# Twelve taps of a depthwise convolution as diagonal matrix products, and a chunk state whose decay is scaled ahead

## The chip, the cores and the metric

The kernel runs on one core of one Trainium2 chip. The metric is the device time of one execution in microseconds (us), taken as the median over several runs. Five engines work from queues of their own, each strictly in the order in which the program was written out: TensorE (PE in the profile, its weight loads PEld), VectorE (DVE), ScalarE (ACT), GpSimd (POOL) and SyncE (SP, which only issues transfers).

## The reference, cut to what matters

Two transformer blocks are computed for 512 tokens of width 1024. The change touches the first half of the first block: a causal depthwise convolution of 31 taps, and a linear recurrence over 16 heads of width 64.

```python
def conformer_conv(val, glu, conv_w, conv_vec):
    u = val * jax.nn.sigmoid(glu)
    y = lax.conv_general_dilated(u, conv_w, window_strides=(1,), padding=[(30, 0)],
                                 dimension_numbers=('NWC', 'WIO', 'NWC'), feature_group_count=1024)
    y = y + conv_vec[0]
    y = layer_norm(y, conv_vec[1], conv_vec[2], LN_EPS)
    return jax.nn.silu(y)

def rwkv7_step(state, inp):
    r_t, w_t, k_t, v_t, kk_t, a_t = inp
    sa = jnp.einsum('bhvk,bhk->bhv', state, -kk_t)
    state = (state * w_t[:, :, None, :] + sa[..., None] * (kk_t * a_t)[:, :, None, :]
             + v_t[..., None] * k_t[:, :, None, :])
    return state, jnp.einsum('bhvk,bhk->bhv', state, r_t)
```

Each channel of the convolution has its own 31 weights; nothing is summed over channels. The rest (attention with an index of selected keys, a short convolution, a large table of experts, a gate) is not touched.

## The kernel before

Channels lie on the 128 partitions and the 512 tokens along the free dimension, so 1024 channels are eight tiles of 128 x 512. The stage in question (function `even`) walks through a list of steps, `ORDER`:

- `A0` to `A7` (`rwkv_a`): the projections r, k, v of one pair of heads, the decays, and the matrices that each chunk of 64 tokens needs.
- `B0` to `B7` (`rwkv_b`): for each pair, a triangular inverse by 31 short steps of a product (line 660) and a reduction (line 662). For pairs 0 and 3 the product is on GpSimd, else on VectorE.
- `C0` to `C7` (`rwkv_c`): the recurrence, eight chunks one after the other. In each chunk PE makes X from the state S of the chunk before (line 705), VectorE copies X (708), PE makes U (712), ScalarE copies U (715), PE makes the new contributions `sy` (718 to 724), and VectorE updates the state: line 730 adds `sy` to S, line 731 multiplies the sum by the chunk's decay `PC`, one scalar per partition. ScalarE then copies the output chunk to `Y` (734).
- `c0` to `c7` (`conv_tile`): one tile of the convolution. Two projections (value and gate) go through PE into banks of PSUM named `mm`, and VectorE makes `u` from them (765), 30 zeros ahead of it. Taps 0 to 10 are multiplied on ScalarE (768 and 771, each 128 x 512 with one scale per partition) and summed on GpSimd into `p2` (772, ten additions). Tap 11 starts `y` on VectorE (778), taps 12 to 30 are added there one by one (780, 19 instructions), and line 783 adds `p2`. The tile goes out to DRAM, and GpSimd keeps a running sum `cs` (787, 789).
- afterwards `n` (normalisation), `g` (gates), `s` and `o` (the first half of the output projection).

All large products split each operand into a high and a low part of a faster 32-bit format, and make three products of them (`product`, lines 216 to 218). Matrices in plain float32 are multiplied without a split; the trace shows such a product of 128 x 512 as two records.

The order of the instructions on each engine is not the written one. A planner in the kernel file (`Order`) builds the program once, estimates each instruction, makes several list schedules of the whole program from priorities of the longest remaining way, and imposes the one with the shortest estimate (`impose`). Any change in one place can thereby move instructions everywhere.

Of the kernel before, what the change touches and what calls it, by code (L numbers as in the profile page):

```python
# [10 lines left out]
F32 = mybir.dt.float32  # L11
# [4 lines left out]
AF = mybir.ActivationFunctionType  # L16
OP = mybir.AluOpType
AX = mybir.AxisListType

T = 512  # L20
# [113 lines left out]
class Net:  # L134
# [253 lines left out]

    NP = 11
    HP = 0  # L390
# [301 lines left out]
    def rwkv_c(self, j):  # L692

        nc, I, wk = self.nc, self.I, self.wk
# [3 lines left out]
        for c in range(8):  # L698
# [27 lines left out]
            if c < 7:  # L726
                S2 = S
                S = wk.tile([128, 64], F32, name="S", bufs=2)
                if c:
                    nc.vector.tensor_tensor(S2, sy[:, 0], S2, OP.add)  # L730
                    nc.vector.tensor_scalar(S, S2, PC[:, c:c + 1], None, op0=OP.mult)
                else:
                    nc.vector.tensor_scalar(S, sy[:, 0], PC[:, c:c + 1], None, op0=OP.mult)
# [24 lines left out]
    def conv_tile(self, j):  # L758
# [6 lines left out]
        nc.vector.scalar_tensor_tensor(u[:, 30:], sg, 1.0, pv, op0=OP.add, op1=OP.mult)  # L765
        NP = self.NP
        p2 = wk.tile([128, T], F32, name="p2")
        nc.scalar.activation(p2, u[:, 0:T], AF.Identity, scale=self.hw[:, 31 * j:31 * j + 1], bias=self.V("conv_b", j))
        for k in range(1, NP):
            pr = wk.tile([128, T], F32, name="pr", bufs=2)  # L770
            nc.scalar.activation(pr, u[:, k:k + T], AF.Copy, scale=self.hw[:, 31 * j + k:31 * j + k + 1])
            nc.gpsimd.tensor_tensor(p2, p2, pr, OP.add)
        y = self.act.tile([128, T], F32, name=f"x{j % 2}")
        if self.CF:
            nc.vector.scalar_tensor_tensor(y, u[:, NP:NP + T], self.hw[:, 31 * j + NP:31 * j + NP + 1], p2,
                                           op0=OP.mult, op1=OP.add)
        else:
            nc.vector.tensor_scalar(y, u[:, NP:NP + T], self.hw[:, 31 * j + NP:31 * j + NP + 1], None, op0=OP.mult)
        for k in range(NP + 1, 31):
            nc.vector.scalar_tensor_tensor(y, u[:, k:k + T], self.hw[:, 31 * j + k:31 * j + k + 1], y,  # L780
                                           op0=OP.mult, op1=OP.add)
        if not self.CF:
            self.eng(5).tensor_tensor(y, y, p2, OP.add)
        nc.sync.dma_start(self.yad[j], y)
# [1120 lines left out]
```

## Time and profile before

| | us |
|---|---|
| median of 3 runs | 2883.79 (2883.66 to 2886.31) |
| the profiled execution | 2893.17 |
| its span, first to last instruction | 2891.4 |
| the stage of the change, 70 to 790 us | 720 |
| PE / DVE / ACT / POOL busy in it | 629 / 537 / 409 / 335 |
| PE clock granted in it, mean | 0.83 of full |

The stage of the change is read here as 70 to 790 us of the span: from the end of the first norm to the end of the eighth recurrence (`C7`). Convolution and recurrences run side by side in it until about 650 us; from 690 us on, gates, output projections and `C7` are left. What follows is the rest of the output projection (to 885), attention (to about 1450), the choice of experts (to 1900) and the experts themselves. The chain of waits that the page shows reaches back over the last 53% of the span only and says nothing of this stage, so the stage has to be read from busy times by stretch, from instruction groups and from waits. PE counts as busy until the modelled end of each product, about 0.2 us longer than the next product has to wait.

### The profile page before, as it was taken

Reading aid. Unit: us, or ns where it says so; the run is one execution under the profiler, and the core shown is the slowest. Engines: PE = TensorE matmul, PEld = TensorE weight load, DVE = VectorE, ACT = ScalarE, POOL = GpSimd, SP = SyncE. Lnnn points to the kernel's source line nnn. Section 1 sums busy time; section 2 is a strip of 40 time slices with the busy share of each in tenths; the row PEclk is TensorE's granted clock in tenths of the full one; section 3 lists DMA queues with packets and bytes.
Section 4 is the critical chain, followed back from the end, with each engine's and each line's share of the span. In section 5 each row is a group of like instructions: output and inputs, shape, how many; then the busy total and the mean of one; then the engine's idle time right before and its main releaser. Section 6 shows DMA issues by size and latency. Waiting matters only on the chain.

```text
span 2891.4 us, 45285 instructions
## 1 busy us (share of the span) xinstructions
PE 2621.8 (91%) x14523; PEld 2231.9 (77%) x14523; DVE 2247.7 (78%) x4338; ACT 1474.0 (51%) x3068; POOL 1852.7 (64%) x1942
## 2 busy tenths in 40 slices
PE   5788998879979999999999988769999999999996
PEld 3656655656757787877878787669999999999995
DVE  6688679896367999973669969978877778788865
ACT  6536546556635538975454347723333444433435
POOL 4535646452245553346657788869988899998963
PEclk9759888888989999999999999979999999999988
DMA  8635444445694231123334366699999999999971
GB/s 264 161 66 118 98 95 107 93 99 126 145 289 143 76 96 44 46 93 105 96 102 148 101 201 245 254 316 337 321 329 314 300 340 339 334 345 320 325 245 64
DMA packets 353440, 552.23 MB, mean 191 GB/s; under 512 B 60081, under 2 KB 239153, under 8 KB 351538
## 3 DMA queue, kind: packets, MB, share of 16 engines
q1 hardware_dynamic: 224690, 295.22, 32.1%
q0 software_dynamic: 64800, 201.88, 23.5%
q10 hardware_dynamic: 63712, 52.24, 5.7%
q8 instruction: 114, 1.87, 0.3%
q14 instruction: 124, 1.02, 0.1%
HBM read 507.76 MB, written 41.42 MB: 190 GB/s over the span
## 4 chain that ended last, share of the span: by engine, by line
PE 31%; DVE 11%; issue 4%; POOL 4%; DMA 2%; ACT 1%; DVEq 0%; POOLq 0%; ACTq 0%; SPq 0%
PE mm L216 5%; PE mm L218 5%; PE mm L217 5%; PE xu L1258 2%; PE xu L1256 2%; PE xu L1257 2%; PE tp L1256 1%; PE tp L1258 1%; POOL wl L209 1%; PE tp L1257 1%; PE nb L1258 1%; PE nb L1256 1%; POOL grow L1330 1%; PE nb L1257 1%; DVE o L1511 1%
## 5 line engine op out<-in xcount | busy, mean ns | idle before, releaser
L209 POOL TENSOR_TENSOR wl<-wraw,wh 128x256 fp32r<-128x256 f32 x937 | 776.7, 846 | 349.3 <-ACT wh L207 290.4
L207 ACT ACTIVATE wh<-wraw 128x256 fp32r<-128x256 f32 x937 | 367.5, 413 | 466.2 <-PE mm L217 235.1
L216 PE MATMUL mm<-xh,wh 128*128 128x352 f32 (+1 forms) x1464 | 512.1, 350 | 11.2 <-DVE wwl L242 3.5
L218 PE MATMUL mm<-xh,wl 128*128 128x352 f32 (+1 forms) x1464 | 506.1, 349 | 6.7 <-POOL wl L209 6.7
L217 PE MATMUL mm<-xl,wh 128*128 128x352 f32 (+1 forms) x1464 | 507.9, 348 | 2.7 <-DVE xl L287 1.8
L216 PEld LDWEIGHTS mm<-xh,wh 128*128 128x128 f32 x1464 | 278.7, 190 | 33.8 <-DVE gate L1544 4.3
L218 PEld LDWEIGHTS mm<-xh,wl 128*128 128x128 f32 x1464 | 277.4, 190 | 26.5 <-POOL wl L209 8.6
L217 PEld LDWEIGHTS mm<-xl,wh 128*128 128x128 f32 x1464 | 278.5, 190 | 24.2 <-DVE xl L287 3.8
L1240 POOL TENSOR_TENSOR vl<-vraw,vh 128x1024 fp32r<-128x1024 f32 x96 | 231.2, 2416 | 6.0 <-ACT vh L1236 4.4
L192 POOL DMA_DIRECT2D dl<-in_wev x114 | 102.4, 917 | 201.7 <-ACT dl L191 180.5
L1345 DVE SCALAR_TENSOR_TENSOR gscr<-grow,wide 128x1024 bf16<-128x1024 f32 x160 | 194.1, 1213 | 38.3 <-DMA grow<-in_ue,gidx 34.8
L216 PE MATMUL mm<-xh,dh 128*128 128x512 f32 x456 | 205.5, 453 | 14.9 <-ACT xh L355 9.6
L1361 DVE SCALAR_TENSOR_TENSOR wide<-grow,gdot,wide 128x1024 f32<-128x1024 f32 x158 | 202.3, 1280 | 12.3 <-DMA grow<-in_ev,gidx 11.2
L217 PE MATMUL mm<-xl,dh 128*128 128x512 f32 x456 | 202.7, 446 | 9.2 <-DVE xl L356 9.2
L218 PE MATMUL mm<-xh,dl 128*128 128x512 f32 x456 | 202.0, 446 | 9.1 <-DMA dl<-in_wev 9.1
L1330 POOL DMA_INDIRECT grow<-in_ue,gidx x160 | 161.1, 1007 | 64.7 <-DVE gscr L1345 31.1
L1256 PE MATMUL xu<-wwh,vh 128*128 128x352 f32 x512 | 167.4, 328 | 32.2 <-ACT wwh L241 28.0
L1330 POOL DMA_INDIRECT grow<-in_ev,gidx x160 | 157.4, 984 | 36.1 <-issue 23.5
L1258 PE MATMUL xu<-wwh,vl 128*128 128x352 f32 x512 | 167.4, 328 | 9.7 <-POOL vl L1240 7.7
L1191 ACT ACTIVATE mm<-mm 128x352 f32<-128x352 f32 x96 | 43.0, 448 | 253.0 <-PE mm L218 211.4
L1257 PE MATMUL xu<-wwl,vh 128*128 128x352 f32 x512 | 167.2, 327 | 0.4 <-DVE wwl L242 0.4
L780 DVE SCALAR_TENSOR_TENSOR x<-u,vec,x 128x512 f32<-128x512 f32 x152 | 165.6, 1089 | 2.4
(575 smaller groups left out, 6961.2 us busy)
## 6 DMA issues: line engine op xcount, KB each, us to landing
vraw<-in_ev SPq DMA_DIRECT2D x128, 512.0 KB
wraw<-in_uT SPq DMA_DIRECT2D x494, 128.0 KB
draw<-in_wev SPq DMA_DIRECT2D x114, 256.0 KB
dl<-in_wev POOLq DMA_DIRECT2D x114, 256.0 KB
gs<-st SPq DMA_DIRECT2D x11, 2048.0 KB
g<-gs ACTq DMA_DIRECT2D x32, 704.0 KB
wraw<-in_wod SPq DMA_DIRECT2D x156, 128.0 KB
adaw<-in_adaT SPq DMA_DIRECT2D x32, 512.0 KB
```

The costliest lines, as they stand in the source:

```text
L207: nc.scalar.activation(wh, raw[:, s], AF.Copy)
L209: nc.gpsimd.tensor_tensor(wl, raw[:, s], wh.bitcast(F32), OP.subtract)
L216: nc.tensor.matmul(ps, wh, xh, start=start, stop=False)
L217: nc.tensor.matmul(ps, wh, xl, start=False, stop=False)
L218: nc.tensor.matmul(ps, wl, xh, start=False, stop=stop)
L1240: nc.gpsimd.tensor_tensor(l, raw, h.bitcast(F32), OP.subtract)
L1256: nc.tensor.matmul(po, vh[i][:, s], wh[i], start=(i == 0), stop=False)
L1257: nc.tensor.matmul(po, vh[i][:, s], wl[i], start=False, stop=False)
L1258: nc.tensor.matmul(po, vl[i][:, s], wh[i], start=False, stop=(i == len(wh) - 1))
L1330: self.nc.gpsimd.indirect_dma_start(out=t, out_offset=None, in_=src, in_offset=bass.IndirectOffsetOnAxis(ap=self.gidx[i][:, k:k + 1], axis=0))
L1345: nc.vector.scalar_tensor_tensor(scr, u, 1.0, x, op0=OP.mult, op1=OP.mult, accum_out=self.gdot[i][:, k:k + 1])
L1361: nc.vector.scalar_tensor_tensor(acc, r, w, acc, op0=OP.mult, op1=OP.add)
```

## The change

`NP` goes from 11 to 12, and the first twelve taps move to PE. ScalarE makes for each tap a diagonal matrix (128 x 128) by scaling the identity with the tap's weight, one scale per partition; four matrices share one buffer, and there are two buffers. PE multiplies each matrix, as plain float32, with the shifted window of `u` and accumulates the twelve products in one bank of `mm`. ScalarE brings the sum out of PSUM with the bias added, as the start of `y`. VectorE then adds taps 12 to 30 as before. The additions on GpSimd, the first tap on VectorE and the final addition of `p2` are gone.

In the recurrence, ScalarE computes `S2`, the old state times the decay, ahead of time; VectorE then makes the new state in one instruction, `sy` times the decay plus `S2`.

```diff
             if c < 7:
-                S2 = S
+                if c:
+                    S2 = wk.tile([128, 64], F32, name="S2", bufs=2)
+                    nc.scalar.activation(S2, S, AF.Copy, scale=PC[:, c:c + 1])
                 S = wk.tile([128, 64], F32, name="S", bufs=2)
                 if c:
-                    nc.vector.tensor_tensor(S2, sy[:, 0], S2, OP.add)
-                    nc.vector.tensor_scalar(S, S2, PC[:, c:c + 1], None, op0=OP.mult)
+                    nc.vector.scalar_tensor_tensor(S, sy[:, 0], PC[:, c:c + 1], S2, op0=OP.mult, op1=OP.add)
...
-        p2 = wk.tile([128, T], F32, name="p2")
-        nc.scalar.activation(p2, u[:, 0:T], AF.Identity, scale=self.hw[:, 31 * j:31 * j + 1], bias=self.V("conv_b", j))
-        for k in range(1, NP):
-            pr = wk.tile([128, T], F32, name="pr", bufs=2)
-            nc.scalar.activation(pr, u[:, k:k + T], AF.Copy, scale=self.hw[:, 31 * j + k:31 * j + k + 1])
-            nc.gpsimd.tensor_tensor(p2, p2, pr, OP.add)
+        NP, ps = self.NP, self.bank("mm")
+        for k0 in range(0, NP, 4):
+            dg = wk.tile([128, T], F32, name="pr", bufs=2).rearrange("p (k c) -> p k c", c=128)
+            for k in range(k0, k0 + 4):
+                nc.scalar.activation(dg[:, k - k0], self.C("ident"), AF.Copy, scale=self.hw[:, 31 * j + k:31 * j + k + 1])
+            for k in range(k0, k0 + 4):
+                nc.tensor.matmul(ps, dg[:, k - k0], u[:, k:k + T], start=(k == 0), stop=(k == NP - 1))
         y = self.act.tile([128, T], F32, name=f"x{j % 2}")
...
-            nc.vector.tensor_scalar(y, u[:, NP:NP + T], self.hw[:, 31 * j + NP:31 * j + NP + 1], None, op0=OP.mult)
-        for k in range(NP + 1, 31):
+        nc.scalar.activation(y, ps, AF.Identity, bias=self.V("conv_b", j))
+        for k in range(NP, 31):
...
-        if not self.CF:
-            self.eng(5).tensor_tensor(y, y, p2, OP.add)
```

In the changed file the new instructions stand on lines 772 (diagonals), 774 (products), 776 (the sum out of PSUM), 729 (`S2`) and 732 (the state); the taps on VectorE are line 778 there and line 780 before, `u` is 766 and 765.

The planner's order changes with it, in three places that matter below. On VectorE, around the making of `u` for convolution tile 3 (`x_3766` and `x_3771` are its `y`). Before:

```order
L675 STREAM_TRANSPOSE T_4047<-Tt 32x256
L765 SCALAR_TENSOR_TENSOR u<-sg,mm 128x512
L778 TENSOR_SCALAR x_3766<-u,vec 128x512
L780 SCALAR_TENSOR_TENSOR x_3766<-u,vec,x_3766 128x512
L730 TENSOR_TENSOR S<-xu,S 128x64
L780 SCALAR_TENSOR_TENSOR x_3766<-u,vec,x_3766 128x512
L731 TENSOR_SCALAR S<-S,PC 128x64
L780 SCALAR_TENSOR_TENSOR x_3766<-u,vec,x_3766 128x512 x2
L708 COPY Xs<-xu 128x64
```

With the change:

```order
L766 SCALAR_TENSOR_TENSOR u<-sg,mm 128x512
L708 COPY Xs<-xu 128x64
L662 TENSOR_REDUCE Tp<-Ltmp 128x8
L660 TENSOR_TENSOR Ltmp<-Tp,Lp 128x8x31
L662 TENSOR_REDUCE Tp<-Ltmp 128x8
L660 TENSOR_TENSOR Ltmp<-Tp,Lp 128x256
L662 TENSOR_REDUCE Tp<-Ltmp 128x8
L732 SCALAR_TENSOR_TENSOR S<-xu,PC,S_3504 128x64
L708 COPY Xs<-xu 128x64
L675 STREAM_TRANSPOSE T_4046<-Tt 32x256 x2
L778 SCALAR_TENSOR_TENSOR x_3771<-u,vec,x_3771 128x512
L732 SCALAR_TENSOR_TENSOR S<-xu,PC,S_3528 128x64
```

Before, the first tap on VectorE stands right behind `u`; with the change nine rows of other work stand between them, and the two state instructions have become one.

On VectorE, at tile 4 (`x_3905` is its `y` in both). Before:

```order
L765 SCALAR_TENSOR_TENSOR u<-sg,mm 128x512
L780 SCALAR_TENSOR_TENSOR x_3766<-u,vec,x_3766 128x512
L778 TENSOR_SCALAR x_3905<-u,vec 128x512
L780 SCALAR_TENSOR_TENSOR x_3905<-u,vec,x_3905 128x512 x2
L730 TENSOR_TENSOR S<-xu,S 128x64
```

With the change:

```order
L778 SCALAR_TENSOR_TENSOR x_3771<-u,vec,x_3771 128x512 x3
L766 SCALAR_TENSOR_TENSOR u<-sg,mm 128x512
L745 SCALAR_TENSOR_TENSOR x_3648<-xu,Y 128x512
L778 SCALAR_TENSOR_TENSOR x_3905<-u,vec,x_3905 128x512 x16
L546 SCALAR_TENSOR_TENSOR k<-mm,om,tm 128x512
```

Here one instruction stands between `u` and the first tap, and 16 taps follow without other work.

On PE, in the recurrence that runs beside convolution tile 3, from one product with S to the contributions `sy`. Before:

```order
L705 MATMUL xu<-S,AR 64x64 x2
L216 MATMUL mm<-xh_103,dh 128x512
L217 MATMUL mm<-xl_111,dh 128x512
L218 MATMUL mm<-xh_103,dl 128x512
L712 MATMUL xu<-Xs,Tt 64x64 x2
L216 MATMUL mm<-xh_104,dh 128x512
L217 MATMUL mm<-xl_112,dh 128x512
L218 MATMUL mm<-xh_104,dl 128x512
L718 MATMUL xu<-UV,BKT 64x64 x2
```

With the change:

```order
L774 MATMUL mm<-u,pr 128x512
L705 MATMUL xu<-S,AR 64x64 x2
L774 MATMUL mm<-u,pr 128x512 x4
L712 MATMUL xu<-Xs,Tt 64x64 x2
L774 MATMUL mm<-u,pr 128x512 x3
L718 MATMUL xu<-UV,BKT 64x64 x2
L721 MATMUL xu<-MT,UV 64x64 x2
L724 MATMUL xu<-AR,S 64x64 x2
```

Where projections filled the gaps of the recurrence, products with the diagonals now do.

## Rows read from the trace of the kernel before

**Rows 1.** By stretch: length, busy (instructions) of PE, PEld, DVE, ACT, POOL; PE clock; DMA.

```profile
70.00:790.00 720.00, 628.79 (x3779) 442.58 (x3778) 537.14 (x1087) 408.53 (x779) 335.13 (x400) 0.83 0.51 110
150.00:240.00 90.00, 79.82 (x468) 54.45 (x467) 69.72 (x182) 36.04 (x74) 28.71 (x44) 0.62 0.35 72
410.00:500.00 90.00, 73.44 (x399) 53.75 (x398) 84.43 (x98) 54.46 (x96) 57.31 (x51) 0.87 0.52 109
690.00:790.00 100.00, 98.11 (x613) 68.62 (x612) 40.57 (x87) 73.06 (x138) 21.62 (x24) 0.93 0.62 132
885.00:1450.00 565.00, 553.37 (x2490) 442.90 (x2488) 457.45 (x817) 348.48 (x727) 279.73 (x325) 0.99 0.27 84
```

**Rows 2.** DVE groups, 70 to 790 us: count | busy us, mean ns | idle before.

```profile
L780 DVE SCALAR_TENSOR_TENSOR x<-u,vec,x 128x512 f32<-128x512 f32 x152 | 165.6, 1089 | 2.4
L731 DVE TENSOR_SCALAR S<-S,PC 128x64 f32<-128x64 f32 x48 | 22.8, 474 | 0.7
L730 DVE TENSOR_TENSOR S<-xu,S 128x64 f32<-128x64 f32 x48 | 10.4, 216 | 23.1 <-PE xu L724 23.0
```

**Rows 3.** POOL groups, 70 to 790 us: the two costliest kinds of addition or product.

```profile
L772 POOL TENSOR_TENSOR p<-p,pr 128x512 f32<-128x512 f32 x80 | 125.0, 1562 | 18.7 <-ACT pr L771 15.2 <-POOL tm L544 0.3
...
L660 POOL TENSOR_TENSOR Ltmp<-Tp,Lp 128x2 f32<-128x2 f32 (+30 forms) x62 | 36.6, 590 | 24.2 <-DVE Tp L662 22.3 <-DVE Xs L708 1.1 <-DVE gpart L439 0.4
```

**Rows 4.** Durations of single lines, ns min/median/max, first and last start.

```profile
L780 DVE SCALAR_TENSOR_TENSOR x<-u,vec,x x152: 730/752/3004, 137.0 to 639.7; 128x512 f32<-128x512 f32 x152
L778 DVE TENSOR_SCALAR x<-u,vec x8: 475/486/1517, 136.5 to 611.3; 128x512 f32<-128x512 f32 x8
L783 DVE TENSOR_TENSOR x<-x,p x8: 680/692/1760, 188.4 to 649.7; 128x512 f32<-128x512 f32 x8
L731 DVE TENSOR_SCALAR S<-S,PC x48: 201/254/1839, 174.6 to 773.8; 128x64 f32<-128x64 f32 x48
L733 DVE TENSOR_SCALAR S<-xu,PC x8: 271/284/285, 167.5 to 746.0; 128x64 f32<-128x64 f32 x8
```

**Rows 5.** Timeline, DVE taps without and with GpSimd's additions: start, us, engine.

```profile
275.86 3.88 DVE L780 SCALAR_TENSOR_TENSOR x<-u,vec,x 128x512 f32<-128x512 f32 x5
413.21 5.78 DVE L780 SCALAR_TENSOR_TENSOR x<-u,vec,x 128x512 f32<-128x512 f32 x4
415.03 3.41 POOL L772 TENSOR_TENSOR p<-p,pr 128x512 f32<-128x512 f32 x2
```

**Rows 6.** Timeline of PE: float32 products of 128x512, at full and half clock.

```profile
688.19 1.12 PE L797 MATMUL nb<-cs,ones 128*128 128x512 f32 x2
689.25 0.33 PE L705 MATMUL xu<-S,AR 64*64 64x64 f32 x4
...
222.81 2.08 PE L748 MATMUL xu<-x,con 128*128 128x512 f32 x2 [3.54 <-ACT x L746]
224.81 1.41 PE L680 MATMUL xu<-T,MT 32*32 32x32 f32 x26
```

**Rows 7.** ScalarE: copies of three sizes; ns min/median/max, or groups as in rows 2.

```profile
L771 ACT ACTIVATE pr<-u,vec 128x512 f32<-128x512 f32 x80 | 55.9, 714 | 13.4 <-POOL p L772 13.2
L768 ACT ACTIVATE p<-u,vec 128x512 f32<-128x512 f32 x8 | 6.5, 809 | 4.0 <-DVE x L783 2.5 <-DVE u L765 1.5
L715 ACT ACTIVATE UV<-xu 64x64 f32<-64x64 f32 x128 | 27.7, 216 | 73.0 <-PE xu L712 71.1
L207 ACT ACTIVATE wh<-wraw x937: 395/417/433, 830.9 to 2860.5; 128x256 fp32r<-128x256 f32 x188
```

**Rows 8.** Waits, 70 to 790 us: who waited for whom, us, times, longest.

```profile
ACT Y L734 <- DVE S L730: 62.1, 37, 3.7
PEld xu L705 <- DVE S L731: 33.7, 28, 3.7
DVE S L730 <- PE xu L724: 23.0, 15, 3.4
```

More of the change, by code (lines that the diff above doesn't have):

```diff
@@ L387, in eng @@
         return self.nc.vector if self.EN[i] == "v" else self.nc.gpsimd
-    NP = 11
+    NP = 12
     HP = 0
@@ L765, in conv_tile @@
         nc.vector.scalar_tensor_tensor(u[:, 30:], sg, 1.0, pv, op0=OP.add, op1=OP.mult)
-        NP = self.NP
-        p2 = wk.tile([128, T], F32, name="p2")
-        nc.scalar.activation(p2, u[:, 0:T], AF.Identity, scale=self.hw[:, 31 * j:31 * j + 1], bias=self.V("conv_b", j))
-        for k in range(1, NP):
-            pr = wk.tile([128, T], F32, name="pr", bufs=2)
-            nc.scalar.activation(pr, u[:, k:k + T], AF.Copy, scale=self.hw[:, 31 * j + k:31 * j + k + 1])
-            nc.gpsimd.tensor_tensor(p2, p2, pr, OP.add)
-        y = self.act.tile([128, T], F32, name=f"x{j % 2}")
[L774 to L777, printed above, removed]
-            nc.vector.tensor_scalar(y, u[:, NP:NP + T], self.hw[:, 31 * j + NP:31 * j + NP + 1], None, op0=OP.mult)
-        for k in range(NP + 1, 31):
+        NP, ps = self.NP, self.bank("mm")
[5 more added lines that the diff above has]
+                nc.tensor.matmul(ps, dg[:, k - k0], u[:, k:k + T], start=(k == 0), stop=(k == NP - 1))
+        y = self.act.tile([128, T], F32, name=f"x{j % 2}")
+        nc.scalar.activation(y, ps, AF.Identity, bias=self.V("conv_b", j))
+        for k in range(NP, 31):
             nc.vector.scalar_tensor_tensor(y, u[:, k:k + T], self.hw[:, 31 * j + k:31 * j + k + 1], y,
                                            op0=OP.mult, op1=OP.add)
-        if not self.CF:
-            self.eng(5).tensor_tensor(y, y, p2, OP.add)
         nc.sync.dma_start(self.yad[j], y)
```

## The prediction, made before the changed kernel ran

> **What bounds the kernel now.** I read the stretches first [rows 1]. From 885 us on PE is busy nearly without a break at full clock, 553 of 565 us in attention, and the change puts nothing there. So only the 720 us of the convolution and recurrence stage count. In these no engine is full: PE 629 us, VectorE 537, ScalarE 409, GpSimd 335, at a PE clock of 0.83. PE works at one of two clocks, 1.2 and 2.4 GHz, so a mean of 0.83 says that it ran about 34% of the time at the lower one. Where PE makes many small products of the recurrences the clock falls to 0.62; where large products dominate (attention) it is 0.99. Beside the convolution tiles VectorE is the fuller engine, 84 of 90 us from 410 to 500, against PE's 73. In the last 100 us it is PE, 98 of 100, and there the change does almost nothing. So VectorE paces the stretch from 70 to 690, and PE is close behind it.
>
> Then I read what VectorE does [rows 2, 4]. Its largest group is the 152 taps of line 780. One takes 752 ns at the median but 1089 on average and up to 3004. The timeline shows why [rows 5]: five taps take 3.88 us (0.78 each) where GpSimd adds nothing, and four take 5.78 us (1.45 each) while two of GpSimd's additions of line 772 run. The 80 additions run over the same stretch as the taps, and they are 125 of GpSimd's 335 us [rows 1, 3]. VectorE's multiplication by the decay shows the same: 254 ns at the median, 474 on average, 1839 at most [rows 2, 4]. The waits say that the recurrence feels it: PE's product with the state stood 33.7 us waiting for line 731 [rows 8].
>
> **The change, part by part.**
>
> VectorE, instructions gone. Per tile the first tap (486 ns) and the last addition (692 ns) [rows 4]: 8 x 1.18 = 9.4 us.
>
> VectorE, state. 48 pairs of 216 + 474 ns go, 33.2 us [rows 2]. The one that takes their place is not in the trace. Nearest below is line 730 (216 ns, no scalar), nearest above the 752 ns of a tap of 512 elements; line 733 has the same size, the same PSUM input and a scalar, 284 ns [rows 2, 4]. I take 284: 13.6 us, so 19.6 us less. This one lies on the recurrence's own path.
>
> VectorE, taps. The excess over the median is 152 x (1089 - 752) = 51 us. Some of it belongs to GpSimd's other work, which stays (line 660, for one, 36.6 us [rows 3]). I take 45; the ends are 0 (nothing comes from line 772) and 51. Together VectorE loses 9.4 + 19.6 + 45 = 74 us, and stands at 463.
>
> The Trainium skill, SBUF — State Buffer, Who interferes with whom, says that a VectorE instruction with two inputs in SBUF and a GpSimd instruction that reads SBUF block each other fully. That agrees with rows 5, and it speaks against counting all of the gain: every GpSimd instruction that reads SBUF would block alike, and by that the remaining ones would keep part of the 51 us, some 20 of it if they reach as many taps. The sum below would then be 23 us in place of 40.
>
> PE. 96 products in float32 come in. One takes 1.06 us at full clock (688.19 to the next start at 689.25) and 2.00 at half (222.81 to 224.81) [rows 6]: 102 to 192 us. I take 102, since twelve large products in a row are the kind of work at which the clock was high. With the clock of the whole stage one takes 1.38 (34% of the time at 2.00), 132 in all. They must fit into PE's idle 91 us and into what the clock gives back. If the clock rises to the 0.93 of the last stretch, the time at half clock falls from 245 us (34% of 720) to about 95 (14% of 680), and each such microsecond returns half: 75 us. PE then needs 629 + 102 - 75 = 656 us of a stage of 680, 96%, just under the 98% that it reaches at the end of the stage. So the products hide behind VectorE, but only with the higher clock.
>
> Latency of the new wait. VectorE's taps of a tile now wait for twelve products and ScalarE's copy out of PSUM: 12 x 1.06 + 0.6 = 13.3 us after `u`. Queued behind the waiting tap stand VectorE's copies of X and the state updates, and PE's recurrence waits for these. By the planned order other VectorE work fills the time: in five tiles 13 to 39 rows. I count 0.75 us for a full-size one [rows 4] and 0.22 to 0.49 for a short one (line 730; the stage's mean, 537 us over 1087 [rows 1, 2]): 11 to 18 us. In tile 3 it is worth about 4 us (four short ones of `B`, two copies, a state update, two transposes), in tile 4 one instruction of 0.8 us, in tile 7 seven instructions, about 5 us. The shortfalls are 9, 12.5 and 8 us, with some 4 us in the other tiles: 34 us in which VectorE stands still. Before, the first tap stood right behind `u`. If the cover of the five also failed, it would cost about 60 us more.
>
> ScalarE. 55.9 + 6.5 us go [rows 7]. 96 diagonals, 48 scaled states and 8 copies come in. From the nearest rows (216 ns for 64 elements, 417 for 256, 714 for 512 with a scale) these are bounded by 96 x 0.22 to 0.71, 48 x 0.22 to 0.71 and 8 x 0.6 to 0.8 us: 36 to 109 us. With 0.42, 0.28 and 0.6 it is 59, so even. By the formula of the Trainium skill's page ScalarE: Activation LUTs (What ACT_TABLE_LOAD costs) the diagonals take 386 ns each and the scaled states 332, which gives 58. ScalarE is busy 409 of 720 us, and this is hidden. The diagonals need only weights, so eight per tile are made before `u`; only the last four wait for a buffer. The copy of line 776 waits for the last product, and behind it on ScalarE stand the next chunk's copies. They wait at most for the last few products, 2 to 4 us per tile, part of the 13.3. `S2` needs the old state only and is due four steps later; it stands behind a copy that waits for the same VectorE instruction anyway (62.1 us over 37 times [rows 8]), so I price it at nothing, at most 48 x 0.7 us if it came late each time.
>
> The bank. The sum occupies one of three turning `mm` banks for about 13 us. The two others cover it; without them PE's projections would stand behind it, up to 8 x 13 us, which belongs to the first rival.
>
> **Sum.** 74 us less on the fuller engine, 34 us of new standstill: 40 us less. The profiled execution took 2893.17 us, 9.4 above the median of 2883.79; I put the difference against the median: 2844. The planner moved instructions after this stage too; there PE is full before and after, and I allow 10 us either way. Own range of this case: 2811 to 2874. The lower end has 51 us from the taps and half the standstill, 63 us less; the upper end has 25 us from the taps, 20 us less; and the allowance on either side.
>
> **Rivals.**
>
> First, PE becomes the bound (slower). The clock stays at 0.83. Then the products cost 132 us; 629 + 132 = 761 us at 98% makes a stage of 776, 56 us more. With the ends of products overlapping better it would be less, so I price it at 40: 2924. It decides as soon as the net addition on PE passes 0.98 x 720 - 629 = 77 us, that is if the clock gives back less than 25 of the 102 us. For it: PE was already busy 87%, and 0.62 shows that small products, which remain, hold the clock down. Against it: twelve dense products per tile. 0.17.
>
> Second, more is gained. VectorE's idle time of 183 us shrinks with its work, because much of it is waiting in the other direction (23.0 us for line 724, for instance [rows 8]), and the standstills fall where PE would have waited anyway: 463 / 537 x 720 = 621, 99 us less: 2785. 0.14.
>
> Third, the change does not relieve what it means to: the long taps come from GpSimd's other work. Then 45 us drop out, 29 - 34 = 5 us more: 2889, no measurable change. For it: other GpSimd work, line 660 above all, runs beside taps too [rows 3]. Against it: rows 5. 0.09.
>
> **How the numbers follow.** The forecast has 0.60. Differences below 0.2% (6 us) can't be told from none. Faster is the forecast but for a small corner, and the second rival: 0.73. Same is the third and that corner: 0.09. Slower is the first, with a little of the third: 0.18. The range reaches from the second rival's 2785 into the first one's beginnings, 2895; outside I leave about half of the first and a few hundredths below.
>
> **What would show it.** The taps' mean falls from 1089 to about 800 ns; GpSimd is busy about 210 us in the stage; the state takes one instruction of about 284 ns, and PE's wait for it falls below 33.7 us. The mean clock beside the convolution tiles reaches 0.9 or more. VectorE stands about 12 us before the first tap of tile 4 and 8 to 9 before tiles 3 and 7. The stage ends 40 us earlier, near 750. I am wrong if the clock stays and PE shows no idle time, if the taps stay long, or if VectorE's standstills add up to the 74 us.

## The result and the profile after

The changed kernel took 2848.16 us (median of 4 runs, 2846.41 to 2857.47), the kernel before, beside it and earlier, 2885.05 us (4 runs, 2883.66 to 2897.88): a ratio of 0.986 with a 95% interval of 0.983 to 0.989, 37 us less. The profiled execution took 2849.02 us with a span of 2847.1.

First the stretches of the kernel after, columns as in [rows 1]: length, busy time (instructions) of PE, PEld, DVE, ACT and POOL, PE clock, DMA. The stage now ends at 754 us, so its line answers to the one from 70 to 790, and 654 to 754 to the one from 690 to 790.

```profile
70.00:754.00 684.00, 652.44 (x3975) 434.20 (x3975) 436.83 (x1021) 394.12 (x844) 217.95 (x322) 0.95 0.54 116
150.00:240.00 90.00, 89.75 (x574) 56.57 (x573) 61.31 (x172) 40.37 (x103) 19.45 (x35) 0.83 0.42 85
410.00:500.00 90.00, 87.84 (x512) 57.09 (x510) 66.21 (x138) 47.99 (x110) 25.53 (x33) 1.00 0.49 105
654.00:754.00 100.00, 98.86 (x672) 67.45 (x671) 50.52 (x123) 73.33 (x152) 22.29 (x26) 1.00 0.61 129
```

The stage is 36 us shorter. VectorE lost 100 us of work (537 to 437), GpSimd 117 (335 to 218). PE gained only 24 (629 to 652) although 96 products came in, since its clock went from 0.83 to 0.95. PE is now busy 95% of the stage, where it was 87%; from 410 to 500 us the fuller engine has changed from VectorE (84 of 90 us) to PE (88 of 90). Of the kernel before, only that stretch and the one behind it have VectorE as the fuller engine. In the others beside the convolution tiles, and over the whole stage (629 against 537), PE already was (before, columns as above):

```profile
240.00:330.00 90.00, 81.43 (x515) 58.33 (x515) 73.56 (x113) 59.93 (x115) 64.85 (x79) 0.92 0.58 121
330.00:410.00 80.00, 74.17 (x519) 48.89 (x519) 54.69 (x147) 38.96 (x86) 28.66 (x48) 0.81 0.40 82
500.00:600.00 100.00, 83.67 (x523) 55.96 (x524) 84.86 (x197) 54.04 (x108) 51.08 (x55) 0.85 0.42 88
600.00:690.00 90.00, 77.32 (x497) 54.94 (x497) 74.12 (x150) 48.80 (x96) 38.21 (x37) 0.84 0.53 120
```

A simple sum helps to read all that follows: the stage is PE's busy time plus PE's idle time. Before it was 629 + 91 us, after it is 652 + 32.

Next the groups on VectorE in the stage (count | busy us, mean ns | idle before and what ended it), which answer to [rows 2], and line 660, which no edit touches:

```profile
L778 DVE SCALAR_TENSOR_TENSOR x<-u,vec,x 128x512 f32<-128x512 f32 x152 | 117.4, 772 | 22.6 <-ACT x L776 21.2
L660 DVE TENSOR_TENSOR Ltmp<-Tp,Lp 128x2 f32<-128x2 f32 (+30 forms) x186 | 63.9, 344 | 18.7 <-POOL Lp L652 15.2
L732 DVE SCALAR_TENSOR_TENSOR S<-xu,PC,S 128x64 f32<-128x64 f32 x48 | 13.4, 280 | 27.4 <-PE xu L724 25.6 <-ACT dl L191 1.8
```

The same 152 taps cost 117 us in place of 166, 772 ns each in place of 1089. They now wait 21.2 us for ScalarE's copy out of PSUM. The state is one instruction of 280 ns in place of 216 + 474. Line 660 fell from 423 ns to 344 without being edited; its group of before reads:

```profile
L660 DVE TENSOR_TENSOR Ltmp<-Tp,Lp 128x2 f32<-128x2 f32 (+30 forms) x186 | 78.8, 423 | 10.3 <-POOL Lp L652 6.2
```

The new instructions of PE and ScalarE, single lines (ns min/median/max, first and last start), beside [rows 6] and [rows 7]:

```profile
L774 PE MATMUL mm<-u,pr x192: 590/592/1221, 132.7 to 604.8; 128*128 128x512 f32 x192
L772 ACT ACTIVATE pr<-con,vec x96: 384/386/403, 112.6 to 592.0; 128x128 f32<-128x128 f32 x96
L729 ACT ACTIVATE S<-S,PC x48: 338/339/348, 173.6 to 730.2; 128x64 f32<-128x64 f32 x48
L776 ACT ACTIVATE x<-mm,vec x8: 672/687/687, 150.4 to 605.5; 128x512 f32<-128x512 f32 x8
```

And the new standstill at tile 4 (tiles counted from 0), in order of time: start, us, engine, and in brackets the idle time before and what ended it. The third line is a run of 20 records of the products, ten products.

```profile
422.93 0.69 DVE L745 SCALAR_TENSOR_TENSOR x<-xu,Y 128x512 f32<-128x512 f32 x1 [2.58 <-PE xu L539]
...
422.73 8.75 PE L774 MATMUL mm<-u,pr 128*128 128x512 f32 x20
...
431.52 0.69 ACT L776 ACTIVATE x<-mm,vec 128x512 f32<-128x512 f32 x1 [2.16 <-PE mm L774]
...
432.24 0.76 DVE L778 SCALAR_TENSOR_TENSOR x<-u,vec,x 128x512 f32<-128x512 f32 x1 [8.61 <-ACT x L776]
```

VectorE finishes a sum of the recurrence at 423.6, and stands until the products and the copy are through at 432.2. The other starts of a tile that wait are 8.47 us (tile 2) and 3.80 (tile 3).

To compare kernels at two points I use one line that all have, the residual sum that closes the even half (line 477 here, the first half of the first block), and its last start. Before and after:

```profile
L477 DVE SCALAR_TENSOR_TENSOR x<-mm,mod,xi x8: 732/740/753, 852.9 to 882.3; 128x512 f32<-128x512 f32 x8
L477 DVE SCALAR_TENSOR_TENSOR x<-mm,mod,xi x8: 737/747/752, 815.8 to 845.5; 128x512 f32<-128x512 f32 x8
```

882.3 against 845.5: the gain of 37 us is there at the end of the stage and its projections. What follows, up to the end of the span, took 2009 us before and 2002 after, with the same instructions.

### The profile page after: what moved, and what is told of

It is laid out like the page before. It is cut to its first block, busy times and chain, and to the rows that moved or that the text cites. A ratio compares the mean times of both kernels' runs of the same rounds, so it can differ in the third digit from the quotient of the medians.

```text
span 2847.1 us, 45547 instructions
## 1 busy us (share of the span) xinstructions
PE 2638.1 (93%) x14715; PEld 2209.6 (78%) x14715; DVE 2125.0 (75%) x4274; ACT 1467.5 (52%) x3135; POOL 1722.0 (60%) x1862
## 4 chain that ended last, share of the span: by engine, by line
PE 59%; DVE 21%; DMA 6%; issue 5%; POOL 4%; ACT 3%; ACTq 0%; SPq 0%; DVEq 0%; POOLq 0%
PE mm L218 11%; PE mm L217 11%; PE mm L216 11%; PE xu L1254 2%; PE xu L1252 2%; PE xu L1253 2%; DVE x L778 2%; PE mm L774 2%; DVE o L1507 1%; DVE Ltmp L660 1%; DVE Tp L662 1%; PE tp L1254 1%; POOL wl L209 1%; PE tp L1253 1%; PE tp L1252 1%
## 5 line engine op out<-in xcount | busy, mean ns | idle before, releaser
L209 POOL TENSOR_TENSOR wl<-wraw,wh 128x256 fp32r<-128x256 f32 x937 | 759.3, 828 | 392.5 <-ACT wh L207 302.4
L216 PE MATMUL mm<-xh,wh 128*128 128x352 f32 (+1 forms) x1464 | 512.2, 352 | 28.9 <-ACT wh L207 12.5
L218 PE MATMUL mm<-xh,wl 128*128 128x352 f32 (+1 forms) x1464 | 507.5, 351 | 13.7 <-POOL wl L209 13.4
L216 PE MATMUL mm<-xh,dh 128*128 128x512 f32 x456 | 198.2, 437 | 10.6 <-ACT xh L355 10.0
L217 PE MATMUL mm<-xl,dh 128*128 128x512 f32 x456 | 194.1, 428 | 8.8 <-DVE xl L356 8.8
L218 PE MATMUL mm<-xh,dl 128*128 128x512 f32 x456 | 192.9, 425 | 6.0 <-DMA dl<-in_wev 6.0
L1253 PE MATMUL xu<-wwl,vh 128*128 128x352 f32 x512 | 165.6, 324 | 0.0
L1232 ACT ACTIVATE vh<-vraw 128x1024 fp32r<-128x1024 f32 x128 | 134.4, 1053 | 50.3 <-DMA vraw<-in_ev 39.0
```

What stands on the lines that cost most here:

```text
L209: nc.gpsimd.tensor_tensor(wl, raw[:, s], wh.bitcast(F32), OP.subtract)
L216: nc.tensor.matmul(ps, wh, xh, start=start, stop=False)
L217: nc.tensor.matmul(ps, wh, xl, start=False, stop=False)
L218: nc.tensor.matmul(ps, wl, xh, start=False, stop=stop)
L1253: nc.tensor.matmul(po, vh[i][:, s], wl[i], start=False, stop=False)
```

## The experiments

The table has the median of all runs of a kernel, and from its one profiled execution the last start of that line (the even half) and the rest of the span behind it. The ratios stand against medians of the kernel before between 2889 and 2892 us that were taken beside the experiments; differences to the changed kernel's 2848 us compare runs taken at different times. One execution is a weak measure: the kernel before spread from 2871 to 2905 us in these runs, and the changed kernel with fewer plans from 2863 to 2902. In the two middle columns the forms also differ by order: the unedited form of before ends its even half between 863 and 882 us, the changed form between 837 and 861 (the last six rows and the first two). Only a difference beyond these ranges can be put down to an edit.

| kernel | median us (runs) | even half | rest | ratio to before |
|---|---|---|---|---|
| before | 2885.05 (4) | 882.3 | 2009 | |
| after | 2848.16 (4) | 845.5 | 2002 | 0.986 [0.983, 0.989] |
| state alone | 2919.57 (6) | 865.9 | 2042 | 1.012 [1.009, 1.014] |
| convolution alone | 2855.07 (4) | 850.3 | 2000 | 0.990 [0.986, 0.993] |
| idle additions | 2909.89 (6) | 883.2 | 2036 | 1.007 [1.004, 1.009] |
| idle products | 2960.13 (4) | 941.9 | 2023 | 1.025 [1.022, 1.028] |
| no products | 2842.53 (1) | 804.5 | 2036 | |
| sum added last | 2871.73 (5) | 861.9 | 2012 | 0.994 [0.992, 0.996] |
| after, fewer plans | 2882.26 (10) | 860.5 | 2032 | 0.998 [0.995, 1.001] |
| before, fewer plans | 2901.45 (10) | 875.7 | 2029 | 1.004 [1.002, 1.006] |
| before form, before ranks | 2877.81 (10) | 866.5 | 2020 | 0.996 [0.994, 0.998] |
| changed form, before ranks | 2867.98 (7) | 836.6 | 2011 | 0.994 [0.991, 0.996] |
| before form, changed ranks | 2875.70 (10) | 862.7 | 2018 | 0.995 [0.993, 0.998] |
| changed form, changed ranks | 2841.75 (4) | 846.9 | 1998 | 0.984 [0.980, 0.988] |

**The state alone.** The kernel before with the new state update and nothing else:

```diff
-                S2 = S
+                if c:
+                    S2 = wk.tile([128, 64], F32, name="S2", bufs=2)
+                    nc.scalar.activation(S2, S, AF.Copy, scale=PC[:, c:c + 1])
...
-                    nc.vector.tensor_tensor(S2, sy[:, 0], S2, OP.add)
-                    nc.vector.tensor_scalar(S, S2, PC[:, c:c + 1], None, op0=OP.mult)
+                    nc.vector.scalar_tensor_tensor(S, sy[:, 0], PC[:, c:c + 1], S2, op0=OP.mult, op1=OP.add)
```

> The kernel before with the new state update alone: the old state is scaled by the decay on ScalarE, VectorE makes the state in one instruction. Theory (VectorE's time paces the stage): 48 pairs of 216 + 474 ns become 48 of 284 ns, 20 us less on the recurrence's own path, so 10 to 20 us faster than before, 2865 to 2875; the taps stay at about 1090 ns and PE's clock in the stage at about 0.83. Rival (the products lift PE's clock, and that clock makes the gain): at most 5 us faster, since nothing is added on PE.

The expectation failed: the kernel was 28 us slower than the one before beside it, not 10 to 20 faster. The even half ended 16 us earlier, but the rest took 33 us more than before. Nothing there was edited. The taps stayed long (1071 ns), as expected, and the clock in the stage was 0.85. The 865.9 us of the even half lie among those that the form of before reaches by order alone (863 to 882), so the run does not show what the state is worth; it shows that an order made anew can cost more than a small edit brings.

**The convolution alone.** The changed kernel with the old state update (the reverse of the edit above).

> The changed kernel with the old state update. Theory: taps at about 0.78 us (45 us less), two instructions per tile gone (9 us less), up to 34 us of new standstill, and the multiplication by the decay short again without the additions on GpSimd (474 to about 254 ns, 10 us less): 25 to 35 us faster than before, 2850 to 2860, and 5 to 10 us slower than the changed kernel. Rival (clock): about the changed kernel's time, 2848, with the clock at 0.95 in the stage.

The median of 2855 us lay in the expected range; the clock in the stage was 0.96, so the run does not decide between the theory and its rival. The even half ended at 850.3, 32 of the 37 us, and the taps took 772 ns. This is 12 us before the earliest that the form of before reaches by order alone, so the convolution carries a gain. The 5 us to the changed kernel are less than orders move that point, so what the state adds is not shown.

**Idle additions.** The changed kernel with ten additions a tile on GpSimd that nobody reads:

```diff
+        p2 = wk.tile([128, T], F32, name="p2")
+        nc.gpsimd.tensor_tensor(p2, u[:, 0:T], u[:, 1:1 + T], OP.add)
+        for k in range(2, 11):
+            nc.gpsimd.tensor_tensor(p2, p2, u[:, k:k + T], OP.add)
```

> The changed kernel with ten additions per tile on GpSimd (two inputs in SBUF, windows of u) whose sum nobody reads; the result of the kernel stays what it is. Theory (the additions made the taps long): the taps' mean rises from about 0.78 us towards 1.09 as far as the additions run beside them, and the time by 15 to 45 us, 2863 to 2893. Rival (clock): taps or not, the products and the clock of 0.95 stay, so the time stays within 6 us of 2848. Rival (the long taps came from GpSimd's other work): taps stay at 0.78 and the time at 2848.

The whole gain was gone: the even half ended at 883.2, like before, and 23 us behind the latest of the changed form's orders. The median of 2910 us is above what was expected (2863 to 2893), since the rest took 34 us more too. The stretch and VectorE's groups:

```profile
70.00:790.00 720.00, 667.19 (x3980) 445.69 (x3981) 480.67 (x1021) 399.12 (x848) 312.56 (x402) 0.93 0.50 110
L782 DVE SCALAR_TENSOR_TENSOR x<-u,vec,x 128x512 f32<-128x512 f32 x152 | 120.1, 790 | 21.2 <-ACT x L780 19.2
L660 DVE TENSOR_TENSOR Ltmp<-Tp,Lp 128x2 f32<-128x2 f32 (+30 forms) x186 | 80.0, 430 | 16.6 <-POOL Lp L652 12.2
```

The taps stayed short, against the expectation: they start only when the products are through, and by then most additions are over. Other VectorE work became longer instead, line 660 from 344 to 430 ns, and VectorE's busy time grew by 44 us, of the 100 that the change took off. This does not hang on the order: in all seven kernels with such additions line 660 took 408 to 437 ns, in the seven without them 342 to 365. So GpSimd's additions cost time on other VectorE lines too, and with them back the gain is gone. How the 36 us of the stage divide is open: PE's idle time grew from 32 to 53 us, its busy time from 652 to 667. The clock stayed at 0.93 (0.95 with the change), so the higher clock alone does not make the gain.

**Idle products.** The kernel before with twelve products a tile that nobody reads:

```diff
+        ps = self.bank("mm")
+        for k in range(12):
+            nc.tensor.matmul(ps, self.C("ident"), u[:, k:k + T], start=(k == 0), stop=(k == 11))
```

> The kernel before with twelve float32 products per tile (identity with the shifted windows of u) into a bank that nobody reads; the result of the kernel stays what it is. They are the changed kernel's PE work without its relief of VectorE. Theory (PE has room once the clock rises, VectorE paces): the clock in the stage rises from 0.83 to 0.9 or more, and the time stays within 10 us of 2885. Rival (the clock makes the gain): 15 to 40 us faster than before. Rival of the prediction (PE is nearly the bound): 20 to 56 us slower.

```profile
70.00:846.00 776.00, 684.62 (x3979) 452.09 (x3979) 539.19 (x1087) 408.97 (x780) 335.96 (x402) 0.90 0.47 103
L783 DVE SCALAR_TENSOR_TENSOR x<-u,vec,x 128x512 f32<-128x512 f32 x152 | 165.9, 1091 | 2.7
```

The time did not stay within 10 us of before, as the first theory had it. The products cost 60 us at the even half's end, with no tap waiting for them, although the clock rose to 0.90. PE's busy time grew by 56 us and the stage by as much; PE's idle time stayed at 91 us. So none of the products went into PE's waits while VectorE's work was as before, though VectorE was busy for only 539 of the 776 us.

**No products.** The changed kernel without the diagonals and products: the first tap is made on ScalarE, and taps 1 to 11 are left out.

```diff
-        NP, ps = self.NP, self.bank("mm")
...
+        NP = self.NP
...
-        nc.scalar.activation(y, ps, AF.Identity, bias=self.V("conv_b", j))
+        nc.scalar.activation(y, u[:, 0:T], AF.Identity, scale=self.hw[:, 31 * j:31 * j + 1], bias=self.V("conv_b", j))
```

> The changed kernel without its diagonals and products: the sum starts from tap 0, made on ScalarE from the window of u, and taps 1 to 11 are left out of the convolution. It is the relief of VectorE alone. Read by the end of the first block's even half (883 us before, 846 with the change). Theory as predicted (the products cost little more than the taps' standstill of 23 us): 815 to 825. Second theory, from the run with products that nobody reads (883 to 943): the products cost about 60 us wherever they stand, PE being all but full: 780 to 795, so the relief alone is 90 to 100 us.

```profile
70.00:712.00 642.00, 586.50 (x3777) 416.45 (x3776) 447.31 (x1022) 365.76 (x746) 215.84 (x320) 0.89 0.57 124
L772 DVE SCALAR_TENSOR_TENSOR x<-u,vec,x 128x512 f32<-128x512 f32 x152 | 119.7, 792 | 4.7 <-ACT x L770 2.5
```

This is a single execution. The even half ended at 804.5, between the two expectations (815 to 825, and 780 to 795). All but diagonals and products is worth 882.3 - 804.5 = 78 us, and these two take back 845.5 - 804.5 = 41. With them the taps wait 19 us more (21.2 against 2.5). PE has 66 us more to do (586 to 652) in a stage 42 us longer, so 24 us of the products go into PE's waits, which shrink from 56 us to 32, and 42 lengthen the stage.

**The sum added last.** The changed kernel, with tap 12 starting the sum on VectorE, and the products' sum and the bias added behind the taps, so that no tap waits for the products:

```diff
-        nc.scalar.activation(y, ps, AF.Identity, bias=self.V("conv_b", j))
-        for k in range(NP, 31):
+        nc.vector.tensor_scalar(y, u[:, NP:NP + T], self.hw[:, 31 * j + NP:31 * j + NP + 1], None, op0=OP.mult)
+        for k in range(NP + 1, 31):
...
+        nc.vector.scalar_tensor_tensor(y, ps, self.V("conv_b", j), y, op0=OP.add, op1=OP.add)
```

> The changed kernel with the products added last: VectorE starts each tile with tap 12 from u at once, adds taps 13 to 30, and then adds the sum of the products and the bias from PSUM in one instruction; ScalarE's copy is gone. No tap waits for PE; VectorE has one more instruction per tile, 8 x 0.49 us, and the bank is held while the taps run. If the standstill before the first tap costs what the prediction said: the even half ends 15 to 25 us earlier than 846. If PE's fullness is the price, not the standstill: 846 within 8 us, or later because of the bank.

It was 24 us slower than the changed kernel, 16 of them in the even half, where 15 to 25 less were expected if the standstill was the price. VectorE's idle time before the taps was gone (2.3 us), but its idle time in the stage was not: 700 - 451 = 249 us, against 247 with the change. Part of it stands at the state's line now, which waits 40 us for PE where it was 26:

```profile
70.00:770.00 700.00, 656.37 (x3973) 440.12 (x3972) 450.81 (x1032) 392.15 (x834) 210.39 (x321) 0.93 0.52 114
L732 DVE SCALAR_TENSOR_TENSOR S<-xu,PC,S 128x64 f32<-128x64 f32 x48 | 13.4, 280 | 39.6 <-PE xu L724 39.6
```

Since orders alone move the even half's end by as much (next), the run does not say what the standstill costs; it says that it was not a price that one can simply take back.

**Other plans.** Both kernels, with their instructions as they are, but the planner choosing among the schedules of two of its four settings:

```diff
-    nc = build(A, Order(build(A)).best()[1])
+    nc = build(A, Order(build(A)).best((20, 50))[1])
```

The changed kernel:

> The changed kernel, same instructions, in another order: the planner chooses among fewer of its schedules (the first two of four weights). It measures what an order alone is worth. As the prediction allowed: within 10 us of 2848. By the run with the new state alone, which gained 16 us up to 883 us and then lost 33 in the instructions that no edit touched: 15 to 50 us either way, most of it after the even half.

The kernel before:

> The kernel before, same instructions, ordered with the same fewer schedules. As the prediction allowed: within 10 us of 2885. If orders alone are worth more: 15 to 50 us either way, most of it after the even half.

The changed kernel lost 34 us against its earlier median, 15 of them in the even half; the kernel before lost 12 against its median beside it, though its even half ended 7 us earlier. Neither stayed within the 10 us that the prediction allowed. An order alone can be worth nearly as much here as the change.

**Form and order crossed.** Four kernels, two forms by two orders. The planner's list schedule runs once with given priorities: an instruction that both kernels have takes its place in the plan of one of them, and the others come right behind what they depend on.

```diff
-    nc = build(A, Order(build(A)).best()[1])
...
+    o0, same0, _ = made(PLAN)
+    rank = {n: k for k, n in enumerate(o0.best()[1])}
+    o1, same1, new = made(MADE)
...
+    key = {b: float(rank[a]) for a, b in zip(same0, same1)}
...
+    nc = build(A, o1.run({n: -k for n, k in key.items()})[1])
```

The form of before on the ranks of before (PLAN = 0, MADE = 0):

> One of four that cross form and order. All four are ordered in one way: every instruction that both kernels have takes the rank that it has in the plan of one of the two kernels, and the others come right after what they depend on. This one is the form of before with the ranks of before; it sets the level of the four. Ranks are not a plan (ties with buffers and engines come out otherwise), so it need not give 2885: 2870 to 2910.

The changed form on the ranks of before (0, 1):

> The changed form with the ranks of the kernel before. Theory 1, that the edits themselves are worth the 36 us that the stage's end showed and the order of the rest adds nothing on balance: 30 to 45 us below the form of before on the same ranks, and the stage's last DVE instruction about 37 us earlier. Theory 2, that a good part of the 37 us is the luck of another order (orders alone moved 16 to 35 us so far): 0 to 20 us below, or up to 60 below if the luck went the other way.

The form of before on the ranks of the changed kernel (1, 0):

> The form of before with the ranks of the changed kernel. Theory 1: the same as the form of before on its own ranks, within 10 us, and 30 to 45 us above the changed form on these ranks. Theory 2: 15 to 35 us below the form of before on its own ranks, since the ranks carry the gain.

The changed form on its own ranks (1, 1):

> The changed form with its own ranks. Theory 1: 30 to 45 us below the form of before on the same ranks. Theory 2: the lowest of the four by 15 us or more, and the form of before on these ranks within 20 us of it. The mean of the two differences between the forms is the edits' own worth, the mean of the two differences between the ranks is the order's.

By medians the changed form is 10 us below the other on the ranks of before and 34 on its own; at the even half's end it is 30 and 16 us ahead. The ranks of the changed kernel are worth 2 us to the old form and 26 to the new one. Neither theory holds whole: theory 1 wanted 30 to 45 on both ranks, theory 2 wanted the old form to gain from the new ranks, and it didn't. The form gains on either order, by less than 37 on average, and its own order suits it. The runs of one of these kernels spread over 10 to 29 us (2850 to 2879 for the changed form on the ranks of before), so single differences of 10 us are weak. The 30 us at the even half on the ranks of before are flattered: the execution read there is the fastest of seven for the changed form and the slowest of ten for the other.

One thing that an order decides can be pointed at. It is PE's first product with the chosen experts, in the profiled executions of the kernel before, and of the two forms on the ranks of before:

```profile
1902.69 0.66 PE L1256 MATMUL xu<-wwh,vh 128*128 128x352 f32 x1 [27.69 <-ACT wwh L241]
...
1892.09 0.66 PE L1294 MATMUL xu<-wwh,vh 128*128 128x352 f32 x1 [29.77 <-ACT wwh L247]
...
1861.09 0.66 PE L1294 MATMUL xu<-wwh,vh 128*128 128x352 f32 x1 [29.73 <-ACT wwh L247]
```

PE stands 28 to 30 us there in one piece. The same wait is 27.4 us in the state-alone kernel. Among PE's waits of the changed kernel for that stage it doesn't stand at all, nor for the old form on the changed ranks, and with the changed form on them it is 1.3 us. It goes with the order, not with the form. But it does not decide the time of the rest: with it the rest took 2009 to 2042 us in the table (before, the state alone, both forms on the ranks of before), without it 1998 to 2036.

## Why the prediction was right, and where it was not

**The time.** 2844 was forecast, 2848.16 came. The sum was 40 us; the stage's end moved by 36 and the median by 37. That it came so close is in part luck. VectorE lost 26 us more than forecast, and its idle time grew by 30 more; the two errors cancelled. And over four pairs of orders the edits are worth some 25 us, not 40 (below).

**The pace.** The prediction took VectorE as the engine that paces the stage from 70 to 690 us, from one stretch of 90 us. That reading does not hold: over the stage PE was the fuller engine before, and when PE alone got more work (idle products), the stage grew by all of it. Rather the two engines wait for each other, and the change shortened PE's part of these waits (91 us idle to 32; its weight loads' wait for the state alone from 33.7 us [rows 8] to 7.4). The part of the prediction that fitted is its account of PE, 656 us of 680.

**VectorE, -74 us.** At the even half's end the kernel without products is 78 us ahead, but that is not VectorE's relief by itself: its PE was busy 42 us less than before too, at a clock of 0.89. By parts of VectorE's own time: the taps' excess gave 48 us (165.6 - 117.4), of 45 taken and 51 possible. The state stands at 13.4 us where 13.6 was taken. But the engine's busy time fell by 100, not 74. The step missed that GpSimd's additions lengthened more than the two lines of [rows 2] with the widest spread: line 660 alone gave 15 us. Not every line gained: the reductions of line 662 took 248 ns before and 250 after. Little of that showed in the stage, since VectorE's idle time grew from 183 us (720 - 537) to 247 (684 - 437), by 64 where 34 was forecast for the taps' waits.

The Trainium skill, SBUF — State Buffer, Who interferes with whom, has VectorE instructions with two inputs in SBUF and GpSimd instructions that read SBUF blocking each other. The idle additions agree with it: line 660, with two such inputs, went from 344 to 430 ns. The estimate that the prediction drew from it, some 20 us of the taps' excess kept by the other GpSimd work, did not come: 152 x (772 - 751) ns = 3 us are left over the median of 751. Its sum for that case was wrong as well: 31 us from the taps in place of 45 would have given 26 us in all, not 23.

**PE, +102 us, hidden only with a higher clock.** The numbers held closely, the hiding did not. The clock was forecast at 0.93 and came at 0.95; PE's busy time in the stage was forecast at 656 us of 680 and came at 652 of 684. One term was too dear: in a run, ten products took 8.75 us, 0.88 each and not 1.06 [rows 6], and the group's busy time is 91 us, of which the clock gave back 68 (629 + 91 - 652). But of the 66 us that the products add to PE's busy time (no products), 42 lengthened the stage; they were not hidden behind VectorE. That the clock alone is not the gain shows in the idle products, 0.90 and 60 us later; their stage of 776 us is the one that the first rival gave for a clock of 0.83.

**The new standstill, 34 us.** It measured 21.2: 8.5, 3.8 and 8.6 us at tiles 2, 3 and 4, and 0.3 at tile 7, where 0 to 4, 9, 12.5 and 8 were forecast. Tile 4 was the place, as read from the order, and it was less, in part because the products were cheaper. Tile 3 was better covered than counted, tile 2, called covered, was not. At tile 7 VectorE did stand, but one instruction earlier: line 546 is ahead of the tap in its queue and waited 10.6 us for a projection. Waits of this kind, before and after (us, times, longest):

```profile
DVE k L546 <- ACT tm L545: 0.4, 2, 0.2
DVE k L546 <- ACT tm L545: 12.0, 3, 10.6
```

Whether the products held up that projection is not shown. As a price for the products, 34 us was close to the 41 that the kernel without them shows, but it is not the same thing: the waits of the taps alone cannot be taken back (the sum added last), and where no tap waits the products cost 60 us (idle products). By PE's time the price is its 66 us of added busy time less the 24 us of its waits that they fill. What of it would go with the taps' standstill is not settled.

**ScalarE even, the bank and S2 at nothing.** The diagonals took 386 ns (420 taken), the scaled states 339 (280 taken), the copies 687: 37.1 + 16.3 + 5.5 = 59 us, as forecast, against 62 that went; ScalarE is at 394 us of 684, after 409 of 720 [rows 1]. The state's wait for line 729 doesn't appear. Who waited for line 732, us and times:

```profile
  ACT Y L735: 44.5, 30
  PEld xu L705: 7.4, 10
  PE xu L705: 3.3, 7
```

ScalarE's wait for the state is down from 62.1 us [rows 8] to 44.5, that of PE's weight loads from 33.7 to 7.4.

By the formula of the Trainium skill, ScalarE: Activation LUTs, What ACT_TABLE_LOAD costs, the diagonals are estimated at 386 ns and the states at 332; the trace has 386 and 339.

**The order of the rest, 10 us either way.** This term was mis-sized. With no edit in it, the rest behind the even half ran from 1998 to 2042 us over single executions of the fourteen kernels (part of which is the spread of executions of one kernel), 7 below before for the changed kernel, 33 above for the state alone. For before and after it came out near even by balance only. The rest from the end of attention on, cut at the last VectorE instruction of the choice of experts (columns as above), before and after:

```profile
1284.00:1871.00 587.00, 539.31 (x2900) 467.44 (x2898) 441.02 (x1232) 311.75 (x756) 424.35 (x460) 0.98 0.46 153
1871.00:2807.00 936.00, 886.42 (x5377) 877.24 (x5377) 744.09 (x1070) 354.23 (x745) 815.92 (x767) 0.97 0.94 322
...
1258.00:1818.00 560.00, 511.53 (x2733) 437.22 (x2731) 442.26 (x1231) 297.72 (x718) 401.86 (x430) 0.99 0.46 149
1818.00:2769.00 951.00, 913.36 (x5572) 901.31 (x5572) 721.53 (x1076) 371.73 (x785) 838.39 (x800) 0.99 0.94 324
```

One part is 27 us shorter, the other 15 longer, and some 170 to 200 PE instructions have crossed the cut. PE's idle time over both fell from 97 us (1523 - 1426) to 86 (1511 - 1425): the standstill of 28 us went, and 17 of it came back as other waits. So the forecast came out right in the stage by its sum, with two terms that missed in opposite directions, and the 7 us of the rest came by no step of it.

**What the edits are worth whatever the order.** Four pairs have the two forms under the same way of ordering: as given, fewer plans, ranks of before, changed ranks. The changed form leads by 37, 19, 10 and 34 us in the medians, 25 on average, and by 37, 15, 30 and 16 us at the end of the even half, 24 on average. So by these pairs some 25 us of the 37 belong to the edits, and the rest may be an order that suits them; with 10 to 37 over four pairs the share is not settled closer than that. PE's busy and idle time in the stage show the same trade in every pair. The rows of the last three pairs, the form of before above the changed one (columns as above):

```profile
70.00:783.00 713.00, 618.12 (x3786) 430.06 (x3785) 529.66 (x1087) 409.33 (x782) 332.06 (x400) 0.85 0.51 112
70.00:763.00 693.00, 655.38 (x3963) 440.68 (x3962) 443.81 (x1022) 398.86 (x845) 216.85 (x321) 0.93 0.52 114
...
70.00:789.00 719.00, 608.36 (x3847) 431.47 (x3847) 535.35 (x1090) 413.08 (x789) 339.61 (x406) 0.88 0.53 116
70.00:759.00 689.00, 647.16 (x4034) 437.56 (x4033) 450.46 (x1025) 402.30 (x852) 213.00 (x325) 0.96 0.55 121
...
70.00:782.00 712.00, 610.13 (x3834) 434.16 (x3835) 534.67 (x1086) 409.82 (x785) 331.07 (x403) 0.88 0.52 115
70.00:766.00 696.00, 649.18 (x4030) 438.19 (x4029) 444.04 (x1022) 403.76 (x852) 212.08 (x325) 0.95 0.54 119
```

With the change PE's idle time falls by 60, 57, 69 and 55 us, and its busy time grows by 24, 37, 39 and 39 (single executions). At the even half's end, too, the four kernels with the changed form (837 to 861 us) all lie before the four with the form of before (863 to 882). So the edits do gain whatever the order: they save PE some 60 us of waiting and cost it some 35 us of work.

**The rivals.** The first, PE as the bound at 2924, fell with the clock at 0.95, though PE is the fuller engine, as it was before. The second, 2785, needed idle time that shrinks with the work; it grew by 64 us. The third fell with the taps at 772 ns. Of the signs named, the stage's end near 750 came at 754; the clock reached 1.00 from 410 to 500 us, but only 0.83 from 150 to 240.

## What to carry to other kernels

Work taken off GpSimd can free VectorE in more lines than those that look long (here line 660 too, 423 to 344 ns), so count the relief over the whole engine. Then put the sum on the fullest engine: here 100 us of VectorE's busy time became 36 us of the stage, because PE waited 60 us less and worked 24 us more. Where a planner or scheduler orders the whole program, an edit comes with a new order everywhere; run both forms under two or three orders before a difference of one per cent is put down to the edit.

## What the runs showed that was not expected

Unedited code took 1998 to 2042 us in one order or another, and a single standstill of PE of 28 to 30 us in it is there or not by the order, without deciding the sum.

The granted clock follows more than the products. Its mean was 0.83 in the stage of before, 0.90 with twelve products a tile that nobody reads, 0.89 with relief and no products, and 0.88 for the form of before on other priorities, with no edit of the work at all:

```profile
70.00:789.00 719.00, 608.36 (x3847) 431.47 (x3847) 535.35 (x1090) 413.08 (x789) 339.61 (x406) 0.88 0.53 116
```

What it has in common with the others is not settled. And products in plain float32 that follow each other without a break cost 0.88 us each (two records) while the granted clock was 1.00, where one alone had taken 1.06 [rows 6].
